# The sample rows' second norm and FFN operands made inside the first FFN pair, and their high and low parts side by side in the output and down projections

## The chip, the cores and the metric

The program runs on one core of a Trainium2 chip. The metric is the device time of one execution in microseconds (us). TensorE (PE) multiplies, VectorE (DVE), ScalarE (ACT) and GpSimd (POOL) work on tiles in on-chip memory, and SyncE (SP) issues most of the DMAs. Each engine runs its own instructions in order; semaphores order them against each other.

## The reference

One step of a one-layer encoder over 2048 prompt frames and 64 sample frames (width 1024). Each frame goes through the same chain, cut here to what matters:

```python
h = rmsnorm(x, g_mix);  z = h @ w_in            # retention heads and softmax (FoX) heads
mix = concat(ret_output(o_r, g_r), o_fox)       # 512 + 512 columns
x = x + mix @ w_out                             # output projection
h = rmsnorm(x, g_ffn)                           # the second norm
x = x + (silu(h @ w_gate) * (h @ w_up)) @ w_down   # D_FF = 2816
y = rmsnorm(x, g_final)
```

The outputs also hold the keys, values and log forget values of all frames and the retention states.

## The kernel before

Everything is float32. A product is made of two-term operands: `split` makes a high part (ACT casts to fp32r, the format that PE multiplies in one pass) and a low part (DVE subtracts), and a product is three matmuls: high by high, high by low, low by high.

The stages, in order of time:

- **Projections** (`prep`, `product`, `parts`, until about 313 us): two passes `p` over eight pairs of 128-frame tiles. `parts(p, i)` turns the queries and keys of tile `i` with PE (into the PSUM tile `tr`), splits them into `qkT`, splits the values into `vt` and stores both (`qk_d`, `v_d`). `qkT` and `vt` have one buffer each (`bufs=1`), so a tile's parts wait until the stores of the tile before have left the buffer.
- **Heads**: `r_stream` (retention; weights `w_2463` and `w_3440` for the first two heads, hidden states `hT`) runs interleaved with `m_stream` (the sample's softmax heads) and then with `f_stream` (the prompt's softmax heads; PE tiles `s`, `t`, `pv`). `run` does the interleaving: every `yield` of the one stream gives time to the other, which pays with the number that it yields. The weights of the third stage of `r_stream` are loaded and split by `mix_gen[2]`; then `p3_stream` follows in the same stream.
- **Output projection** (`p3_stream`): for each of 17 tiles (16 prompt tiles, and tile 16 with the 64 sample rows and 64 rows of padding) 48 matmuls with `mm<-w,mT`, the residual sum into `x`, the norm (`norm`: ACT squares, POOL makes the factor `r`, DVE scales into `h`), and, one tile later, `back`: eight transposes `rt<-ident,h`, copies into `hT`. After every second tile, and after tile 16 alone, `operands` makes the seven sums and differences that the FFN's products of two halves need and stores them (`h2_d`, in the trace `h_d`); for the first block they are split at once into `hb_t`. The stores wait in the list `late` and go through POOL's DMA queue.
- **FFN** (`prep`, `gu`, `down`, `finish`): three blocks of frames, `BLOCKS = ((768, 768), (0, 768), (1536, 576))`, and for each block 11 pairs `i` of 256 hidden columns. In a pair `gu(i, 0)` makes the gate half (seven products `j` of 12 matmuls `mm<-hb,w`; seven in place of eight, by sums of operands), then `down(i - 1)` the down projection of the pair before (tiles of 128 frames, twelve matmuls `dn<-wd,act` each), then `gu(i, 1)` the up half. `prep(x)` makes the weights of product `x` four products ahead; PSUM tile `b` of a product is shared by some `j`, so a later `j` waits until DVE or ACT has read the earlier one. The last block holds 512 prompt frames and the 64 sample rows: its halves are 288 columns wide, and its fifth down tile has 64 rows only. `finish` norms a tile of the result `y` and stores it.

The order on each engine is that of the code as a scheduler lays it out from the order in which the streams are emitted; pools with few buffers set who waits for whom. On SP all loads stand in one queue.

Of the kernel before, what the change touches and what calls it, by code (L numbers as in the profile page):

```python
# [9 lines left out]
F32 = mybir.dt.float32  # L10
# [6 lines left out]
D = 1024  # L17
# [21 lines left out]
def hybrid_kernel(ctx: ExitStack, tc: tile.TileContext, a: dict):  # L39
# [151 lines left out]
    with tc.tile_pool(name="p1w", bufs=1) as p1w, tc.tile_pool(name="p1", bufs=2) as p1, \  # L191
# [177 lines left out]
        def parts(p, i):  # L369
# [13 lines left out]
            qkT = p1.tile([128, 2, 4, 128], F32R, tag="qkT", name="qkT", bufs=1)  # L383
# [6 lines left out]
            vt = p1.tile([128, 4, 2, DH], F32R, tag="vt", name="vt", bufs=1)  # L390
# [116 lines left out]
        for e in range(2):  # L507
            parts(1, 2 * prev[1] + e)
# [11 lines left out]
    def r_stream():  # L520
# [160 lines left out]

    def p3_stream(last):

        m_t, mT_t, x_t, h_t, rb_t = {}, {}, {}, {}, {}
        hT_b, late = [], []
# [23 lines left out]
        def halves(i):  # L709
# [16 lines left out]
        def back(i):  # L726
# [9 lines left out]
            if i == NT - 1:  # L736
                operands(i // 2, hT[:, :, 0:NS // 2], hT[:, :, NS // 2:NS])
            elif i % 2:
                operands(i // 2, *hT_b[-2:])
            p3_done.add(i)  # L740

        def operands(j, b1, b2):

            w = b1.shape[2]
            lo, hi = slice(0, 4), slice(4, 8)
            t = p3.tile([128, D], F32, tag="h", name="t", bufs=2).rearrange("p (k t) -> p k t", k=KT)[:, :, 0:w]

            def out(n, src):
                if (0, n) in hb_t and j in range(p0, p1):
                    q = slice((j - p0) * 128, (j - p0 + 1) * 128)  # L750
                    split(hb_t[0, n][:, 0, :, q], hb_t[0, n][:, 1, :, q], src)
                    return
                stored.add(j)
                late.append(lambda: dma(h2_d[n, :, :, j * 128:j * 128 + w], src, ge))

            out(0, b1[:, lo])
            out(2, b1[:, hi])
            out(6, b2[:, hi])
            ve.tensor_tensor(t[:, lo], b2[:, lo], b1[:, lo], op=ALU.subtract)
            ve.tensor_tensor(t[:, hi], b2[:, hi], t[:, lo], op=ALU.subtract)  # L760
            ve.tensor_tensor(b2[:, lo], b2[:, hi], b2[:, lo], op=ALU.subtract)
            out(4, t[:, lo])
            out(1, t[:, hi])
            out(3, b2[:, lo])
            t4 = p3.tile([128, 4, 128], F32, tag="t4", name="t4", bufs=1)[:, :, 0:w]
            ve.tensor_tensor(t4, t[:, hi], b1[:, hi], op=ALU.subtract)
            out(5, t4)
            if j == NT // 2:
                for o in late:
                    o()  # L770

        def products(mT, c):
            ps = rps.tile([128, 512], F32, tag="mm", name="mm")
            for q in range(4):
                for k in (2 * q, 2 * q + 1):
                    for j, (u, v) in enumerate(((0, 0), (0, 1), (1, 0))):
                        te.matmul(ps, mT[:, u, k], mix_w[4 + c][:, v, k], start=k == 0 and j == 0, stop=k == 7 and j == 2)  # L777
                yield ps
# [7 lines left out]
        for c in range(2):  # L786
            for q, ps in enumerate(products(mT, c)):
# [5 lines left out]
        with tc.tile_pool(name="p3", bufs=2, reuse_waits="tile") as p3:  # L793
# [5 lines left out]
            for i in range(NT):  # L799
# [7 lines left out]
                for c in range(2):  # L807
                    for q, ps in enumerate(products(mT, c) if i else early[c:c + 1]):
# [10 lines left out]
                for o in late:  # L819
                    o()  # L820
# [695 lines left out]
```

## Time and profile before

| what | value |
|---|---|
| median of 3 runs | 2978.17 us (2974.83 to 2978.39) |
| the profiled execution | 2976.43 us, of which the span of the profile is 2974.7 us |
| granted TensorE clock | 0.99 of full speed, mean |
| PE busy | 2873.8 us of the span |
| DVE, ACT, POOL busy | 2114.5, 1308.3, 434.3 us |
| projections until | about 313 us |
| FFN from | about 1527 us |

Times in the rows are counted from the start of the span. A row of the timeline is: start, duration, engine, line, operation, output and inputs, form, count, and in brackets the idle time of the engine ahead of it and what ended that. A row of the windows is: the stretch, its length, the busy time of PE, PEld (weight loads), DVE, ACT and POOL with their counts, the granted clock, the DMA engines' busy share and their rate. Matmuls overlap in the pipeline, so what one costs in a row of them is the distance of the starts, not its own duration.

### The profile page before, as it was taken

How to read it: one execution, taken by the hardware profiler on the slowest of the kernel's cores; microseconds unless marked ns; L12 is line 12 of the kernel's file. 1: busy time of each engine (PE TensorE's matmuls, PEld its weight loads, DVE VectorE, ACT ScalarE, POOL GpSimd, SP SyncE). 2: the span in 40 equal slices, each digit the busy share in tenths (PEclk: the TensorE clock that was granted, in tenths of full speed). 3: DMA queues.
4: the chain of work that ended last, by engine and by line, in shares of the span. 5: the costliest groups of instructions: out<-in, count | busy, mean ns of one | idle time of the engine just before them, and what ended most of it. 6: DMA issues, size and time to landing. Idle time of an engine off the chain costs nothing.

```text
span 2974.7 us, 44950 instructions
## 1 busy us (share of the span) xinstructions
PE 2873.8 (97%) x16440; PEld 2591.4 (87%) x16440; DVE 2114.5 (71%) x4142; ACT 1308.3 (44%) x2765; POOL 434.3 (15%) x611
## 2 busy tenths in 40 slices
PE   7999899999999999899989999999999999999998
PEld 7999688888888888678779999998899999888887
DVE  7887644476766666766647777778777777888886
ACT  6554332265655555654333323335333333533333
POOL 2100111211111111111131011011110110211111
PEclk9999999999999999999989999999999999999999
DMA  6876633332431222554462222216222221622321
GB/s 199 271 227 189 168 106 106 102 104 72 139 90 55 72 87 87 164 157 124 143 215 85 71 58 85 70 58 203 84 85 69 59 78 52 213 86 85 86 86 61
DMA packets 408016, 338.50 MB, mean 114 GB/s; under 512 B 24138, under 2 KB 353226, under 8 KB 407794
## 3 DMA queue, kind: packets, MB, share of 16 engines
q1 hardware_dynamic: 402322, 317.07, 36.1%
q0 software_dynamic: 5472, 18.55, 1.9%
q8 instruction: 130, 2.13, 0.3%
q14 instruction: 92, 0.75, 0.1%
HBM read 255.65 MB, written 79.89 MB: 113 GB/s over the span
## 4 chain that ended last, share of the span: by engine, by line
PE 44%; DVE 3%; issue 2%; DMA 1%; POOL 1%; ACT 1%; POOLq 0%; SPq 0%; ACTq 0%; DVEq 0%
PE mm L1365 25%; PE dn L1394 16%; PE mm L777 3%; DVE w L87 1%; DMA hb<-h_d 0%; DMA raw<-w_up 0%; DVE o L1406 0%; PE rt L732 0%; DVE hb L87 0%; DVE y L1395 0%; POOL r L106 0%; POOL s L1286 0%; POOL s L1287 0%; DVE G L1338 0%; DMA o_yp<-o 0%
## 5 line engine op out<-in xcount | busy, mean ns | idle before, releaser
L1365 PE MATMUL mm<-hb,w 128*128 128x384 f32 (+1 forms) x5544 | 902.5, 324 | 15.8 <-DVE G L1338 11.9
L1365 PEld LDWEIGHTS mm<-hb,w 128*128 128x128 f32 x5544 | 894.1, 189 | 23.8 <-issue 15.2
L1394 PE MATMUL dn<-wd,act 128*128 128x512 f32 (+1 forms) x2244 | 517.6, 391 | 4.7 <-ACT act L86 2.7
L1394 PEld LDWEIGHTS dn<-wd,act 128*128 128x128 f32 (+1 forms) x2244 | 413.9, 185 | 98.1 <-ACT act L86 3.5
L662 PE MATMUL mm<-w,hT 128*128 128x512 f32 x1600 | 438.2, 407 | 9.8 <-DVE qkT L87 9.8
L1395 DVE TENSOR_TENSOR y<-y,dn 128x512 f32<-128x512 f32 (+1 forms) x374 | 255.4, 685 | 162.0 <-PE dn L1394 161.7
L662 PEld LDWEIGHTS mm<-w,hT 128*128 128x128 f32 x1600 | 285.4, 190 | 61.1 <-issue 10.5
L87 DVE TENSOR_TENSOR w<-raw,w 128x512 fp32r<-128x512 f32 (+1 forms) x350 | 302.5, 878 | 43.5 <-ACT w L86 37.9
L86 ACT CAST w<-raw 128x512 fp32r<-128x512 f32 (+1 forms) x350 | 215.9, 644 | 200.5 <-PE mm L1365 119.7
L291 PE MATMUL mm<-w,o 128*128 128x386 f32 x1260 | 239.2, 346 | 5.5 <-DVE z L302 3.9
L86 ACT CAST wd<-rawd 128x512 fp32r<-128x512 f32 x132 | 75.7, 619 | 380.2 <-PE dn L1394 377.7
L1092 ACT ACTIVATE P<-P,nm 128x512 f32<-128x512 f32 (+3 forms) x288 | 189.6, 661 | 101.4 <-DVE nm L1086 100.8
L291 PEld LDWEIGHTS mm<-w,o 128*128 128x128 f32 x1260 | 222.4, 191 | 9.5 <-DVE z L302 6.8
L1286 POOL TENSOR_TENSOR s<-raw 128x512 f32<-128x512 f32 x33 | 67.2, 2037 | 1074.2 <-DVE w L87 1040.6
L777 PE MATMUL mm<-w,mT 128*128 128x512 f32 x816 | 209.7, 405 | 6.3 <-DVE x L817 5.8
L86 ACT CAST hi<-t 128x512 fp32r<-128x512 f32 (+1 forms) x288 | 154.6, 561 | 127.9 <-PE t L1109 124.4
L87 DVE TENSOR_TENSOR lo<-t,hi 128x512 fp32r<-128x512 f32 (+1 forms) x288 | 182.8, 655 | 33.7 <-ACT hi L86 32.2
L777 PEld LDWEIGHTS mm<-w,mT 128*128 128x128 f32 x816 | 151.4, 191 | 39.3 <-DVE x L817 6.9
L1109 PE MATMUL t<-ident,P 128*128 128x128 f32 x1088 | 159.7, 275 | 6.3 <-DVE lo L87 4.9
L1125 PE MATMUL pv<-hi,V 128*128 128x256 f32 x576 | 153.2, 291 | 4.4 <-DVE o L1134 2.5
L1109 PEld LDWEIGHTS t<-ident,P 128*128 128x128 f32 x1088 | 127.1, 141 | 28.4 <-DVE lo L87 9.1
L1126 PE MATMUL pv<-lo,V 128*128 128x256 f32 x576 | 145.9, 287 | 2.4 <-DVE lo L87 1.8
(263 smaller groups left out, 3980.4 us busy)
## 6 DMA issues: line engine op xcount, KB each, us to landing
raw<-w_gate SPq DMA_DIRECT2D x66, 512.0 KB
raw<-w_up SPq DMA_DIRECT2D x66, 512.0 KB
rawd<-w_down SPq DMA_DIRECT2D x66, 512.0 KB
hT<-hT_d SPq DMA_DIRECT2D x46, 512.0 KB
x<-x_prompt SPq DMA_DIRECT2D x32, 512.0 KB
qk_d<-qkT SPq DMA_DIRECT2D x64, 256.0 KB
KA<-qk_d SPq DMA_DIRECT2D x72, 128.0 KB
V<-v_d SPq DMA_DIRECT2D x36, 256.0 KB
```

What stands on the lines that cost most here:

```text
L86: se.copy(hi, src)
L87: ve.tensor_tensor(lo, src, f32(hi), op=ALU.subtract)
L291: te.matmul(ps, o[:, u, k], w[:, v, k], start=b == j and k == 0 and m == 0, stop=j not in (0, 4) and k == 3 and m == 2, skip_group_check=True)
L662: te.matmul(ps, hT[:, u, k], w[:, v, k], start=k == 0 and j == 0, stop=k == 7 and j == len(terms) - 1)
L777: te.matmul(ps, mT[:, u, k], mix_w[4 + c][:, v, k], start=k == 0 and j == 0, stop=k == 7 and j == 2)
L1092: se.activation(v, v, AF.Exp, bias=nm, scale=-1.0, accum_out=sum_t[h, u // 4][:, i % 8, ch:ch + 1])
L1109: te.transpose(tr[:, c * 128:(c + 1) * 128], P_t[n, e, j // 2][:, k * 128:(k + 1) * 128], ident)
L1125: te.matmul(o, V, hi[:, p], start=j == 0 and c == 0, stop=False)
L1126: te.matmul(o, V, lo[:, p], start=False, stop=j == u and c == 1)
L1365: te.matmul(ps, w[:, u, k], hb_t[n, j][:, v, k, 0:hf], start=b == j and k == 0 and m == 0, stop=j not in (0, 4) and k == 3 and m == 2, ski ...
L1394: te.matmul(ps, act_t[i][e][:, u, f:f + m], w[c][:, v, e], start=e == 0 and j == 0, stop=e == 1 and j == 2)
L1395: ve.tensor_tensor(y[:, d], y[:, d], ps, op=ALU.add)
```

## The change

- The last pair's `parts` of the projections take buffers of their own (`slots`: the tiles of four `o` operands that are no longer needed) and go in the order second tile, first tile.
- The last four steps of `mix_gen[2]` each yield 1500, so that time is given back to the other stream between them.
- In the output projection tile 16 holds the high parts of its 64 rows in columns 0 to 63 and the low parts in columns 64 to 127 (`halves_beside`): two matmuls instead of three, and `add_low` adds the lower half of the PSUM tile to the upper.
- The norm, the transposes and `operands` of tile 16 leave `p3_stream`. The new `sample_operands` does them in `gu(0, 0)`, one step ahead of each of `j` = 3 to 6; it reads `x1_d` and the gain again, in six `y` tiles. The loads of `y` for the first block's results (`load_y`) follow its last step.
- In `prep(0)` the first weights are split ahead of the sums of the weights.
- In the down projection of the last block the 64-row tile holds high and low parts side by side, two matmuls instead of three; `gu` splits each result in two pieces (256 and 32 columns), `load_y` clears the lower half of `y`, `finish` adds the lower half to the upper.

```diff
-        def parts(p, i):
+        def parts(p, i, slots=None):
...
-            qkT = p1.tile([128, 2, 4, 128], F32R, tag="qkT", name="qkT", bufs=1)
+            if slots is None:
+                qkT = p1.tile([128, 2, 4, 128], F32R, tag="qkT", name="qkT", bufs=1)
+                vt = p1.tile([128, 4, 2, DH], F32R, tag="vt", name="vt", bufs=1)
+            else:
+                qkT, vt = (p1w.tile([128, 2, 4, 128], F32R, tag=f"o{n}", name="last") for n in slots)
+                vt = vt[:, 0].rearrange("p h (s d) -> p h s d", s=2)
...
-        for e in range(2):
-            parts(1, 2 * prev[1] + e)
+        for e in (1, 0):
+            parts(1, 2 * prev[1] + e, (2 * e, 2 * e + 1))
...
         for _ in range(4):
             next(mix_gen[2])
+            yield 1500
         yield from p3_stream([lambda f=f: f(prev) for f in (step_T, step_A, step_O, step_M)])
...
-                split(mT[:, 0, s], mT[:, 1, s], m[:, s])
+                if i == 16:
+                    halves_beside(mT[:, 0, s], m[:, s])
+                else:
+                    split(mT[:, 0, s], mT[:, 1, s], m[:, s])
...
-        def products(mT, c):
+        def products(mT, c, i):
+            terms = ((0, 0), (0, 1), (1, 0))[0:2 if i == 16 else 3]
...
+                    if i == 16:
+                        add_low(ps, p3.tile([128, 512], F32, tag="t4", name="t16", bufs=1)[0:NS])
                     ve.tensor_tensor(x[:, d], ps, x[:, d], op=ALU.add)
-                norm(i, x)
-                for o in late:
-                    o()
-                late.clear()
-            yield from back(NT - 1)
+                if i < 16:
+                    norm(i, x)
+                else:
+                    dma(x1_d[SEQ:TP], x, ge)
+                write_late()
...
             if j == 0:
...
+                if x == 0:
+                    split(o[:, 0], o[:, 1], r0[:, lo])
                 en = ge if s else ve
...
-            full = [(t0 + 128 * m, 128, m // 2 * 128 + m % 2 * (hf + tail // 2)) for m in range(nt // 128)]
+            full = [(t0 + 128 * m, 128, m // 2 * 128 + m % 2 * (hf + 2 * tail)) for m in range(nt // 128)]
...
+            if m < 128:
+                ge.memset(y[m:2 * m], 0.0)
             dma(y[0:m], x1_d[t:t + m])
...
-                split(o[:, 0, c:c + hf - tail], o[:, 1, c:c + hf - tail], g[:, 0:hf - tail])
+                split(o[:, 0, c:c + full], o[:, 1, c:c + full], g[:, 0:full])
                 if tail:
-                    split(o[:, 0, hf:c], o[:, 1, hf:c], g[:, hf - tail:hf])
+                    c = full + tail * (q % 2)
+                    split(o[:, 0, c:c + tail], o[:, 0, c + 2 * tail:c + 3 * tail], g[:, full:hf])
...
+                terms = ((0, 0), (0, 1), (1, 0))[0:3 if m == 128 else 2]
...
-            y = y_t.pop(t)[0:n]
+            yy = y_t.pop(t)
+            y = yy[0:n]
             o = fw.tile([128, D], F32, tag="rawd", name="o", bufs=2)[0:n]
+            if n < 128:
+                se.copy(o, yy[n:2 * n])
+                ve.tensor_tensor(y, y, o, op=ALU.add)
...
+        def sample_operands():
+
+            x, g, h, hT, t, t4 = (fw.tile([128, D], F32, tag="y", name="y", bufs=6) for _ in range(6))
+            dma(x, x1_d[SEQ:TP])
+            dma(g, a["norm_ffn_gain"].to_broadcast([128, D]))
+            yield
+            r = rms_scale(fw, x, h, 128, 2)
+            ve.scalar_tensor_tensor(h, x, r, g, op0=ALU.mult, op1=ALU.mult)
+            yield
+            hT = hT.rearrange("p (k t) -> p k t", k=KT)
+            for g in range(2):
+                tr = ps4.tile([128, 512], F32, tag="dn", name="tr").rearrange("p (k t) -> p k t", k=4)
+                for k in range(4):
+                    te.transpose(tr[:, k], h[:, (4 * g + k) * 128:(4 * g + k + 1) * 128], ident)
+                se.copy(hT[:, 4 * g:4 * g + 4], tr)
+            yield
+            operands(NT // 2, hT[:, :, 0:NS // 2], hT[:, :, NS // 2:NS], t, t4[:, 0:512])
+            for t, m, _ in tiles(0):
+                load_y(t, m)
+            yield
...
-        for t, m, _ in tiles(0):
-            load_y(t, m)
+        first = sample_operands()
...
             for j in gu(i, 0):
+                if i == 0 and j >= 3:
+                    next(first)
```

`operands` moves out of `p3_stream` unchanged in what it computes, with the two scratch tiles as arguments.

On SP, where the projections end and the heads begin, before (`vt` and `qkT` are the buffers of the parts, `rot`, `tri`, `nmask` and `self` are constants, `raw<-w_in` are the last two quarters of the weights `w_3440`, `o_lfp` the output of the log forget values):

```order
L48 DMA cg<-c_gam 128x16
L48 DMA rot<-c_rot 128x128
L48 DMA raw<-w_in 128x2x256
L48 DMA qk_d<-qkT 128x4x128 x2
L48 DMA v_d<-vt 128x4x128
L48 DMA raw<-w_in 128x2x256 x3
L48 DMA rot<-c_rot 128x128
L48 DMA qk_d<-qkT 128x4x128 x2
L48 DMA v_d<-vt 128x4x128
```

The same place now:

```order
L48 DMA qk_d<-last 128x4x128 x4
L48 DMA rmask<-c_rmask 128x512
L48 DMA cg<-c_gam 128x16
L48 DMA o_lfp<-lf 128x16x8
L48 DMA o_lfs<-lf 64x8
L48 DMA tri<-c_tri 128x128
L48 DMA nmask<-c_nmask 128x64
L48 DMA self_3413<-c_sel 40x512
L48 DMA rot<-c_rot 128x128
L48 DMA raw<-w_in 128x2x256 x4
```

The last stores of the parts moved ahead of the constants, and the four weight loads moved behind the store of the forget values and four constants.

On PE at the same place, before (`tr` the last turns of the parts, `s<-ident,A` turns for the sample's heads, `w_2463` and `w_3440` the two weight tiles of the first retention tile):

```order
L375 MATMUL tr<-ident,z 128x128 x8
L884 MATMUL s<-ident,A_941 8x128 x4
L662 MATMUL mm<-w_2463,hT 128x512 x6
L884 MATMUL s<-ident,A_941 8x128 x4
L662 MATMUL mm<-w_2463,hT 128x512 x11
L884 MATMUL s<-ident,A_941 8x128 x4
L662 MATMUL mm<-w_2463,hT 128x512
```

The same place now:

```order
L375 MATMUL tr<-ident,z 128x128 x8
L899 MATMUL s<-ident,A_941 8x128 x4
L666 MATMUL mm<-w_2463,hT 128x512 x6
L899 MATMUL s<-ident,A_941 8x128 x4
L666 MATMUL mm<-w_2463,hT 128x512 x18
L666 MATMUL mm<-w_3440,hT 128x512 x11
L899 MATMUL s<-ident,A_941 8x128 x4
```

Eleven matmuls of the second weight tile moved ahead of the turns `s<-ident,A`.

On PE where the output projection ends and the FFN begins, before (`w_14160` is the second weight tile of the projection, `rt` the turns of `h`; the rows `rt` behind the first FFN row are those of tile 16):

```order
L777 MATMUL mm<-w_14160,mT 128x512 x18
L732 MATMUL rt<-ident,h 128x128 x4
L777 MATMUL mm<-w_14160,mT 128x512 x4
L732 MATMUL rt<-ident,h 128x128 x4
L777 MATMUL mm<-w_14160,mT 128x512 x2
L1365 MATMUL mm<-hb,w 128x384 x12
L732 MATMUL rt<-ident,h 128x128 x8
L1365 MATMUL mm<-hb,w 128x384 x240
```

The same place now (`tr<-ident,y` are the turns of tile 16):

```order
L789 MATMUL mm<-w_13989,mT 128x512 x16
L789 MATMUL mm<-w_14160,mT 128x512 x12
L774 MATMUL rt<-ident,h 128x128 x4
L789 MATMUL mm<-w_14160,mT 128x512 x4
L774 MATMUL rt<-ident,h 128x128 x4
L1389 MATMUL mm<-hb,w 128x384 x84
L1453 MATMUL tr<-ident,y 128x128 x8
L1389 MATMUL mm<-hb,w 128x384 x168
```

The turns of tile 16 moved behind the whole gate half of the first pair, and tile 16 has 32 matmuls where it had 48. On SP the six loads of `y` moved with them:

```order
L48 DMA raw<-w_up 128x8x128 x2
L48 DMA y<-x_d 128x1024
L48 DMA raw<-w_gate 128x8x128 x2
L48 DMA y<-norm_ffn_gain 128x1024
L48 DMA rawd<-w_down 128x2x512 x2
L48 DMA y<-x_d 128x1024 x6
L48 DMA raw<-w_up 128x8x128 x2
```

The six loads stood directly behind the first two `raw<-w_up` before; now they stand between the first `rawd<-w_down` and the second pair's `raw<-w_up`, and a load of the sample's rows and one of the gain stand ahead.

More of the change, by code (lines that the diff above doesn't have):

```diff
@@ L676, in r_stream, with write_late, operands, out @@
             next(mix_gen[2])
+            yield 1500
         yield from p3_stream([lambda f=f: f(prev) for f in (step_T, step_A, step_O, step_M)])
     f_done = set()
+    def write_late():
+        for o in late:
+            o()
+        late.clear()
+    def operands(j, b1, b2, t, t4):
+        w = b1.shape[2]
+        lo, hi = slice(0, 4), slice(4, 8)
+        t = t.rearrange("p (k t) -> p k t", k=KT)[:, :, 0:w]
+        t4 = t4.rearrange("p (k t) -> p k t", k=4)[:, :, 0:w]
+        def out(n, src):
+            if (0, n) in hb_t and j in range(p0, p1):
+                q = slice((j - p0) * 128, (j - p0 + 1) * 128)
+                split(hb_t[0, n][:, 0, :, q], hb_t[0, n][:, 1, :, q], src)
+                return
+            stored.add(j)
+            late.append(lambda: dma(h2_d[n, :, :, j * 128:j * 128 + w], src, ge))
+        out(0, b1[:, lo])
+        out(2, b1[:, hi])
+        out(6, b2[:, hi])
+        ve.tensor_tensor(t[:, lo], b2[:, lo], b1[:, lo], op=ALU.subtract)
+        ve.tensor_tensor(t[:, hi], b2[:, hi], t[:, lo], op=ALU.subtract)
+        ve.tensor_tensor(b2[:, lo], b2[:, hi], b2[:, lo], op=ALU.subtract)
+        out(4, t[:, lo])
+        out(1, t[:, hi])
+        out(3, b2[:, lo])
+        ve.tensor_tensor(t4, t[:, hi], b1[:, hi], op=ALU.subtract)
+        out(5, t4)
+        if j == NT // 2:
+            write_late()
     def p3_stream(last):
         m_t, mT_t, x_t, h_t, rb_t = {}, {}, {}, {}, {}
-        hT_b, late = [], []
+        hT_b = []
         def load_m(i):
@@ L735, in back @@
             hT_b.append(hT)
[L736 to L739, printed above, removed]
+            if i % 2:
+                operands(i // 2, *hT_b[-2:], p3.tile([128, D], F32, tag="h", name="t", bufs=2),
+                         p3.tile([128, 512], F32, tag="t4", name="t4", bufs=1))
             p3_done.add(i)
[L742 to L768, printed above, removed]
-                for o in late:
-                    o()
-        def products(mT, c):
+        def products(mT, c, i):
+            terms = ((0, 0), (0, 1), (1, 0))[0:2 if i == 16 else 3]
             ps = rps.tile([128, 512], F32, tag="mm", name="mm")
@@ L775, in products @@
                 for k in (2 * q, 2 * q + 1):
-                    for j, (u, v) in enumerate(((0, 0), (0, 1), (1, 0))):
-                        te.matmul(ps, mT[:, u, k], mix_w[4 + c][:, v, k], start=k == 0 and j == 0, stop=k == 7 and j == 2)
+                    for j, (u, v) in enumerate(terms):
+                        te.matmul(ps, mT[:, u, k], mix_w[4 + c][:, v, k], start=k == 0 and j == 0,
+                                  stop=k == 7 and j == len(terms) - 1)
                 yield ps
@@ L786, in p3_stream @@
         for c in range(2):
[L787 removed]
+            for q, ps in enumerate(products(mT, c, 0)):
                 if q % 2 == 0:
```

36 lines of the change are left out of this document (19 added, 17 removed).

## The prediction

> **What bounds the kernel now.** I read the page first, its busy times and its chain, then the groups of waits, then the timeline of the four places that the change touches.
>
> ```profile
> PE 2873.8 (97%) x16440; PEld 2591.4 (87%) x16440; DVE 2114.5 (71%) x4142; ACT 1308.3 (44%) x2765; POOL 434.3 (15%) x611
> PE 44%; DVE 3%; issue 2%; DMA 1%; POOL 1%; ACT 1%; POOLq 0%; SPq 0%; ACTq 0%; DVEq 0%
> ```
>
> PE is busy for 2873.8 of 2974.7 us and has the largest part of the chain. So time can be won in two ways only: by fewer matmuls, or out of the 100.9 us in which PE idles. Everything off PE counts where it makes PE wait, and at the very end.
>
> **The last parts of the projections.** The only wait of the first retention matmuls stands here:
>
> ```profile
> 323.36 2.90 PE L662 MATMUL mm<-w,hT 128*128 128x512 f32 x6 [9.85 <-DVE qkT L87]
> 316.53 1.60 SPq L48 DMA_DIRECT2D qk_d<-qkT  x2
> 321.14 0.38 ACT L384 ACTIVATE qkT<-tr 128x256 fp32r<-128x256 f32 x1 [4.89 <-DVE p L848]
> 318.49 1.16 DVE L87 TENSOR_TENSOR w<-raw,w 128x1024 fp32r<-128x1024 f32 x1
> 318.77 2.27 SPq L48 DMA_DIRECT2D raw<-w_in  x3
> 323.03 1.05 ACT L86 CAST w<-raw 128x1024 fp32r<-128x1024 f32 x1 [0.34 <-DMA raw<-w_in]
> 325.95 0.38 SPq L48 DMA_DIRECT2D o_lfp<-lf  x1
> 326.38 1.30 SPq L48 DMA_DIRECT2D o_lfs<-lf  x1
> 328.37 0.47 SPq L48 DMA_DIRECT2D tri<-c_tri  x1
> 313.00:323.00 10.00, 0.51 (x5) 0.17 (x2) 9.14 (x20) 2.85 (x7) 5.47 (x11) 0.71 0.97 269
> 325.00:327.00 2.00, 2.00 (x8) 1.26 (x8) 1.89 (x4) 1.40 (x2) 0.00 (x0) 0.50 0.97 256
> 327.00:329.00 2.00, 2.00 (x9) 1.64 (x9) 1.87 (x12) 0.57 (x1) 0.00 (x0) 0.87 0.66 63
> ```
>
> PE idles from 313.51 to 323.36. The single `qkT` is stored at 316.53, refilled only from 321.14, and PE comes after its split; meanwhile DVE works at the sample's softplus (`p`) and the weights. With buffers of their own the last parts (about 0.4 us each on DVE and ACT, as the 0.38 of the copy) should be through at about 316.5: PE starts 6.9 us earlier. But the order now puts the last four loads of `w_3440` behind `o_lfp`, which waits for `lf`, the end of the softplus. `lf` comes earlier too: 2.4 us of weight splits (two like the 1.16) move behind it and about 0.9 of DVE's 10 us were idle, so `o_lfp` goes at about 322.6. Behind it stand five small transfers (`o_lfs` 1.30, the constants 0.4 to 0.5 like `tri`, about 3.1 us), so the loads go at about 326; from issue to the cast it took 323.03 - 318.77 = 4.3 us, with cast and split (1.05 + 1.16) the third quarter is ready at about 332. PE gets there after 36 matmuls and 20 small turns, 316.5 + 36 x 0.235 + 1.8 + 2 for a half clock = about 329. A wait of some 2.5 us comes back: 6.9 - 2.5 = 4.4, **taken -4.5**; ends 0 (the loads land so late that all is given back) and -9.5 (no wait is left).
>
> **The four yields.** They move projection matmuls against the end of the prompt's softmax heads.
>
> ```profile
> 1200.00:1230.00 30.00, 21.90 (x129) 17.86 (x128) 25.57 (x64) 22.25 (x48) 3.54 (x6) 0.94 0.57 171
> 1230.00:1300.00 70.00, 61.18 (x335) 49.85 (x334) 41.13 (x104) 34.72 (x84) 6.85 (x14) 0.98 0.55 151
> 1229.28 0.40 PE L777 MATMUL mm<-w,mT 128*128 128x512 f32 x1
> L1126 PE MATMUL pv<-lo,V x576: 272/281/562, 601.3 to 1394.3; 128*128 128x256 f32 x189, 128*128 128x128 f32 x3
> ```
>
> PE idles 8.1 us of the first stretch (27%) and 8.8 of the second; the first projection matmul comes at 1229.28 and the softmax runs to 1394.3. The order still mixes the two streams and puts the first projection matmuls a little later. I see no reason for a sign: **taken 0**, ends -8 (half of the 16.9 idle) and +6 (three quarters of one more stretch of 8.1).
>
> **Output projection and start of the FFN.**
>
> ```profile
> 1502.89 10.50 PE L777 MATMUL mm<-w,mT 128*128 128x512 f32 x44
> 1527.58 2.25 PE L1365 MATMUL mm<-hb,w 128*128 128x384 f32 x12
> 1533.11 1.11 PE L732 MATMUL rt<-ident,h 128*128 128x128 f32 x4 [3.28 <-DVE h L722]
> 1534.94 1.11 PE L732 MATMUL rt<-ident,h 128*128 128x128 f32 x4 [0.72 <-ACT hT L733]
> 1537.11 1.65 PE L1365 MATMUL mm<-hb,w 128*128 128x384 f32 x4 [1.06 <-ACT U L1368]
> 1539.43 2.93 PE L1365 MATMUL mm<-hb,w 128*128 128x384 f32 x8 [0.68 <-ACT w L86]
> 1541.52 9.38 PE L1365 MATMUL mm<-hb,w 128*128 128x384 f32 x50
> 1553.84 16.35 PE L1365 MATMUL mm<-hb,w 128*128 128x384 f32 x77 [2.94 <-DVE G L1338]
> 1541.60 0.99 SPq L48 DMA_DIRECT2D raw<-w_up  x2
> 1562.80 0.99 SPq L48 DMA_DIRECT2D raw<-w_up  x2
> 1553.80:1556.00 2.20, 2.16 (x7) 2.19 (x8) 1.56 (x3) 1.90 (x4) 0.00 (x0) 0.50 1.15 317
> ```
>
> Tile 16 loses 16 matmuls; 44 take 10.50 us and overlap a little at the end, so 0.235 each: -3.8. From 1527.58 to 1541.52, 13.9 us, PE does 24 FFN matmuls and the eight turns, with 3.28 + 0.72 + 1.06 + 0.68 us of waits. Now the turns go and with them the wait for the norm: 24 x 0.188 (9.38 / 50) = 4.5 us, the wait for `U` and for the next split as before (1.74), and about 1.8 for DVE, which has the halves' sum and the residual of tile 16 (two additions like the y additions, 0.7) ahead of the splits: 8.0. That is -5.9. The eight turns come later, at 1.1 us (the two rows show 1.11 each, at half clock): +1.1. The stores and loads come later as well. The second `raw<-w_up` was issued at 1562.80; now it stands behind six loads of `y`, which wait for the sample's stores, at an estimate some 8 us later and about when the second pair needs its first split: +1. The first `raw<-w_up` (1541.60) keeps its place behind POOL's stores, so the wait of 2.94 stays. Cover of the sample's norm and sums: the gate half's matmuls; DVE carries them, and it is DVE that PE waits for at 1553.84. Sum -3.8 - 5.9 + 1.1 + 1 = **-7.6**; ends -11 and -3. The split of the first weights ahead of their sums goes with it, at nothing of its own; 0.68 (`ACT w`) is its most.
>
> The clock is a cost of its own: after 9.85 us of waiting it stood at 0.50 until about 327.5, after 2.94 us it stood at 0.50 too, but not everywhere:
>
> ```profile
> 2602.00:2604.00 2.00, 2.00 (x10) 1.62 (x11) 2.00 (x4) 0.00 (x0) 0.00 (x0) 1.00 0.00 0
> 2601.82 8.49 PE L1394 MATMUL dn<-wd,act 128*128 128x512 f32 x36 [2.01 <-DVE y L1395]
> ```
>
> A wait of 2.01 us left it at 1.00. So I take half clock for waits of 2.9 and more and full clock at 2.0. The Trainium skill's page "TensorE: Matmul & The Clock Gate", section "Part 1: The HAM clock gate (the "warmup" mystery)", has the gate close after an idle window of about 3.4 us. The row of 2.94 contradicts it as a limit on one wait. By the rule, a new wait of 2.5 to 2.9 us costs only itself and the total would be about 2 us lower; by the rows it can cost up to 2 us more.
>
> **The down projection of the last block.**
>
> ```profile
> 2669.33 13.82 PE L1394 MATMUL dn<-wd,act 128*128 128x512 f32 x60
> 2682.99 20.70 PE L1365 MATMUL mm<-hb,w 128*128 128x288 f32 x156
> 2704.07 1.82 PE L1365 MATMUL mm<-hb,w 128*128 128x288 f32 x12 [0.39 <-DVE G L1338]
> 2689.83 0.45 DVE L87 TENSOR_TENSOR act<-G,act 128x288 fp32r<-128x288 f32 x1
> 2692.62 0.53 DVE L87 TENSOR_TENSOR act<-G,act 128x256 fp32r<-128x256 f32 x2
> L1394 PEld LDWEIGHTS dn<-wd,act 128*64 128x64 f32 x132 | 17.7, 134 | 11.9
> L1394 PEld LDWEIGHTS dn<-wd,act 128*128 128x128 f32 x2112 | 396.1, 188 | 86.2 <-ACT act L86 3.5 <-DVE y L1395 2.4 <-DVE act L87 0.2
> ```
>
> 60 matmuls stand between 2669.33 and 2682.99: 0.2277 each. Four fewer per pair are 0.91 us; ten of the eleven pairs lie in this row's manner between PE's other work, the last is counted with the end: -9.1. The narrow tile's weights get 128 columns: 88 loads of 188 ns are 16.5 us, where 132 of 134 were 17.7, and both hide under 0.2277. Two more results per pair are split in two pieces (0.53 where 0.45 stood): 0.16 us of DVE per pair. It lies in the up half; where DVE is late (PE's 0.39) it can reach PE, so +0.5 over all of 1.8 at most. **-8.6**, ends -9.5 and -5 (a wait of 0.4 more in every pair). The POOL `memset` of half of `y` stands ahead of a load that is needed a block's first pair later; POOL is 15% busy: 0, and with its cover gone at most about 1.3, what the 64x1024 below takes on DVE.
>
> **The end.**
>
> ```profile
> 2967.39 1.06 ACT L102 ACTIVATE o<-y 64x1024 f32<-64x1024 f32 x1 [3.34 <-DMA o_yp<-o]
> 2969.46 1.28 DVE L1406 SCALAR_TENSOR_TENSOR o<-y,r,gfin 64x1024 f32<-64x1024 f32 x1 [2.92 <-POOL r L106]
> ```
>
> The last tile's square waits for the buffer `o` (3.34 us, for a store) and nothing hides what follows. A copy like 1.06 and an addition like 1.28 come behind that wait: +2.34, with hand-overs **+2.4**. Its ends are +1 (the four fewer matmuls of the last pair, 0.9, bring part of it forward) and +3.
>
> **Sum.** -4.5 + 0 - 7.6 - 8.6 + 2.4 = -18.3. On the profiled execution's 2976.43 us this is 2958.1. The median of the runs shown is 2978.17, 1.7 higher, so I say 2959, between the two.
>
> **Rivals.**
>
> 1. More comes from the yields. PE's 16.9 us of idling at the end of the softmax are halved: -8, time 2951, and with better ends elsewhere 2941 to 2951. For it: projection matmuls are ready work there. Against it: the first ones come later than before.
>
> 2. The start of the FFN turns into a new wait. The sample's norm and sums (1.28 for a scaling of 64x1024, and seven sums) go on DVE in just the stretch where PE waits 2.94 us for DVE; and SP's queue holds back `raw<-w_up`, each us of lateness a us of PE, with half clock behind it. 3 us at the first, 3 at the second, with 2 for the clock: +8, time 2967; 2965 to 2972. For it: DVE is the releaser in both waits. Against it: the same DVE work stood in the 14 us before.
>
> 3. About the same, 2972 to 2984: the terms of the down projection and of tile 16 stand (-12.4), but the loads of `w_3440` give back more than the buffers won (+4.5 over 0) and the FFN's start too. Time 2974.
>
> 4. Slower, over 2984, by one mechanism: with time given back to the softmax between the last steps, the projection's matmuls come so late that the softmax runs alone. Alone it idles 27% (1200 to 1230). To eat the 18.3 us and 7 more takes 25 / 0.27 = 92 us alone: no projection matmul before 1229 + 92 = 1321. Against it: the order still interleaves them from the beginning.
>
> 5. That the change doesn't do what it says: a wait stays at the `tr` of the parts, since their PSUM tiles and DVE are the old ones. Then -4.5 becomes 0: 2963, inside the range.
>
> **How the numbers follow.** A run of this kernel tells 0.2%, 6 us, from no change, so "same" is 2972 to 2984. The forecast, 2951 to 2965: 0.57. Rival 1: 0.11. Rival 2: 0.18. Rival 3: 0.10. Rival 4: 0.04. Rival 5 lies in the forecast. Faster is 0.57 + 0.11 + 0.18 = 0.86. The range, 2949 to 2971, leaves out most of rival 1, rivals 3 and 4, and a little of rival 2: about 0.2.
>
> **What the profile after would show.** The wait of 9.85 us at the first retention matmul falls to about 3, and a new one of 2 to 3 stands behind the first half of `w_3440`, released by the DVE or ACT split. The two stretches from 1200 keep about 17 us of idling. No turn of `h` stands between the FFN's first matmuls; the first 24 take about 8 us. A `dn` row of one pair has 56 matmuls in 12.75 us. At the end a copy and an addition stand ahead of the last square. I am wrong if the new operands make PE wait over 5 us for `G` or `w` in the first two pairs, or if the softmax's end shifts by more than 8 us.

## The result and the profile after

The changed kernel took 2956.1 us (median, 2955.22 to 2956.78), the kernel before 2978.28 us beside it: a ratio of 0.9924, 95% interval 0.9908 to 0.994. The forecast was 2959, range 2949 to 2971. The profiled execution took 2955.22 us, its span is 2953.4 us; that is 21.3 us less than the span before.

The page after, busy times and chain:

```profile
PE 2859.6 (97%) x16380; PEld 2584.8 (88%) x16380; DVE 2121.6 (72%) x4167; ACT 1310.6 (44%) x2790; POOL 436.8 (15%) x612
PE 42%; DVE 5%; issue 2%; DMA 2%; POOL 1%; ACT 0%; SPq 0%; POOLq 0%; DVEq 0%; ACTq 0%
```

PE is busy 14.2 us less and idle 93.8 us instead of 100.9. The 60 matmuls that are gone (16 and 44) make about two thirds of the gain. Of the 7.1 us less idling, 5.8 lie between 1200 and 1515 us (21.1 us before, 15.4 now), where PE's idle time differs by as much between runs with the same yields, as the experiments show. So this trace alone doesn't show that the change won them.

Where the heads begin, the timeline after, and then the window 313 to 345 of before and of after:

```profile
314.57 2.46 PE L666 MATMUL mm<-w,hT 128*128 128x512 f32 x6 [1.63 <-DVE x L853]
324.28 1.19 PE L666 MATMUL mm<-w,hT 128*128 128x512 f32 x4 [0.23 <-DVE w L87]
329.37 1.20 PE L899 MATMUL s<-ident,A 128*8 128x128 f32 x8 [0.83 <-DVE arow L903]
333.09 0.66 PE L575 MATMUL rt<-ident,qk 128*128 128x128 f32 x4 [1.44 <-POOL qk L551]
319.75 0.40 SPq L48 DMA_DIRECT2D o_lfp<-lf  x1
323.23 1.91 SPq L48 DMA_DIRECT2D raw<-w_in  x4
322.46 1.74 DVE L87 TENSOR_TENSOR w<-raw,w 128x1024 fp32r<-128x1024 f32 x1
330.55 1.22 DVE L87 TENSOR_TENSOR w<-raw,w 128x1024 fp32r<-128x1024 f32 x1
```

```profile
313.00:345.00 32.00, 22.09 (x128) 15.86 (x126) 23.84 (x54) 12.39 (x22) 7.50 (x14) 0.84 0.73 193
```

```profile
313.00:345.00 32.00, 26.91 (x148) 19.07 (x149) 23.51 (x52) 14.10 (x25) 9.62 (x14) 0.95 0.54 146
```

The wait of 9.85 us is one of 1.63, and PE starts 8.8 us earlier. But a row of small waits follows: for the split of `w`, for `arow` (the turns of `A`), for POOL's rotation. The split that PE waits for at 324.28 was begun at 322.46, before the last four loads were issued at 323.23; theirs is begun at 330.55, and no row shows PE waiting for it. In the 32 us PE idles 5.1 us where it idled 9.9, so nearly half of the gain is gone within some 20 us.

Where the FFN begins, the timeline after; the last row is the first down projection of before:

```profile
1516.23 2.33 PE L1389 MATMUL mm<-hb,w 128*128 128x384 f32 x12
1525.01 1.65 PE L1389 MATMUL mm<-hb,w 128*128 128x384 f32 x4 [6.44 <-ACT U L1392]
1527.93 14.70 PE L1389 MATMUL mm<-hb,w 128*128 128x384 f32 x68 [1.28 <-ACT w L86]
1543.59 29.42 PE L1389 MATMUL mm<-hb,w 128*128 128x384 f32 x168
1572.85 16.51 PE L1419 MATMUL dn<-wd,act 128*128 128x512 f32 x72
1523.87 0.58 ACT L95 COPY t<-mm 64x512 f32<-64x512 f32 x1 [6.64 <-DMA h_d<-t]
1519.62 0.92 POOL L48 DMA_DIRECT2D h_d<-t  x1
1523.21 2.36 SPq L48 DMA_DIRECT2D raw<-w_up  x2
```

```profile
1587.90 16.50 PE L1394 MATMUL dn<-wd,act 128*128 128x512 f32 x72
```

From the FFN's first matmul to the first down projection it is 56.6 us (1572.85 - 1516.23) instead of 60.3 (1587.90 - 1527.58). The turns of `h` and the wait for the norm are gone, and so is the wait of 2.94 us; but a new wait of 6.44 us stands for the copy of `U`. ACT names its cause one row on: the copy in `add_low` (L95) stands ahead of that of `U` in ACT's queue, and it waits 6.64 us for the store `h_d<-t`. Its scratch tile has the tag `t4`, one buffer, and that buffer still holds the last operand of the prompt's frames, whose store POOL issued at 1519.62. The first `raw<-w_up` went out 7.0 us behind the FFN's first matmul (1523.21); before it was 14.0 us (1541.60 - 1527.58).

The softmax of the prompt ended earlier, at 1384.4 us instead of 1394.3:

```profile
L1141 PE MATMUL pv<-lo,V x576: 272/281/583, 599.7 to 1384.4; 128*128 128x256 f32 x189, 128*128 128x128 f32 x3
```

The last block's down projection, and the end:

```profile
2652.71 12.90 PE L1419 MATMUL dn<-wd,act 128*128 128x512 f32 x56
2688.29 12.89 PE L1419 MATMUL dn<-wd,act 128*128 128x512 f32 x56
2651.05 1.82 PE L1389 MATMUL mm<-hb,w 128*128 128x288 f32 x12 [0.45 <-DVE G L1360]
2925.43 13.05 PE L1419 MATMUL dn<-wd,act 128*128 128x512 f32 x56
2943.40 1.04 ACT L1431 COPY o<-y 64x1024 f32<-64x1024 f32 x1 [2.85 <-DMA o_yp<-o]
2944.48 1.22 DVE L1432 TENSOR_TENSOR y<-y,o 64x1024 f32<-64x1024 f32 x1 [1.40 <-ACT o L1431]
2945.79 1.06 ACT L102 ACTIVATE o<-y 64x1024 f32<-64x1024 f32 x1 [1.34 <-DVE y L1432]
```

A pair takes 35.58 us (2688.29 - 2652.71). PE's wait for `G` grew from 0.39 to 0.45. The last copy still waits for a store, then copy, addition and square follow one another with nothing beside them.

### The profile page after: what moved, and what is told of

Read it like the earlier page. It is cut to its first block, busy times and chain, and to the rows that moved or that the text cites. A ratio compares the mean times of both kernels' runs of the same rounds, so it can differ in the third digit from the quotient of the medians.

```text
span 2953.4 us, 44888 instructions
## 1 busy us (share of the span) xinstructions
PE 2859.6 (97%) x16380; PEld 2584.8 (88%) x16380; DVE 2121.6 (72%) x4167; ACT 1310.6 (44%) x2790; POOL 436.8 (15%) x612
## 4 chain that ended last, share of the span: by engine, by line
PE 42%; DVE 5%; issue 2%; DMA 2%; POOL 1%; ACT 0%; SPq 0%; POOLq 0%; DVEq 0%; ACTq 0%
PE mm L1389 23%; PE dn L1419 16%; PE mm L789 3%; DVE w L87 2%; DMA hb<-h_d 1%; DMA raw<-w_up 0%; DVE act L87 0%; DVE G L1365 0%; DVE o L1436 0%; DMA o_yp<-o 0%; DVE hb L87 0%; DVE y L1421 0%; DVE raw L1311 0%; PE rt L774 0%; POOL r L106 0%
## 5 line engine op out<-in xcount | busy, mean ns | idle before, releaser
L1389 PEld LDWEIGHTS mm<-hb,w 128*128 128x128 f32 x5544 | 893.7, 189 | 27.3 <-issue 13.5
L1419 PE MATMUL dn<-wd,act 128*128 128x512 f32 x2200 | 506.9, 390 | 3.4 <-ACT act L86 2.9
L1419 PEld LDWEIGHTS dn<-wd,act 128*128 128x128 f32 x2200 | 411.8, 188 | 88.7 <-ACT act L86 3.8
L1421 DVE TENSOR_TENSOR y<-y,dn 128x512 f32<-128x512 f32 x374 | 255.4, 686 | 156.5 <-PE dn L1419 155.9
L789 PE MATMUL mm<-w,mT 128*128 128x512 f32 x800 | 202.6, 401 | 2.9 <-DVE x L832 2.5
```

What stands on the lines that cost most here:

```text
L1389: te.matmul(ps, w[:, u, k], hb_t[n, j][:, v, k, 0:hf], start=b == j and k == 0 and m == 0, stop=j not in (0, 4) and k == 3 and m == 2, ski ...
L1419: te.matmul(ps, act_t[i][e][:, u, f:f + 128], w[c][:, v, e], start=e == 0 and j == 0, stop=e == 1 and j == len(terms) - 1)
L1421: ve.tensor_tensor(y[:, d], y[:, d], ps, op=ALU.add)
```

## The experiments

Beside the next runs the kernel before took 2983 to 2985 us, some 6 us more than beside the first, so kernels are compared by their ratio to it. The intervals are about 0.13% wide on each side, 4 us; where less matters, the stretches of the trace decide. The changed kernel was run again for that:

> The changed kernel once more, on the chip of the next three, so that they are compared with it there. It takes 0.9908 to 0.994 of the time of the kernel before, as it did. In the profile the wait for U at the FFN's first matmuls is 6.4 us again, and no wait of 2.9 us for G follows it.

It took 2965.83 us, 0.9939 (0.9926 to 0.9952). The wait for `U` was 6.42 us, and a wait of 1.46 us stood at the sample's turns. The two ratios of the changed kernel are 0.0015 apart, 4.5 us, with intervals that overlap. The differences given below are from the second, unless the first is named.

### The parts: back to single buffers

```diff
-        for e in (1, 0):
-            parts(1, 2 * prev[1] + e, (2 * e, 2 * e + 1))
+        for e in range(2):
+            parts(1, 2 * prev[1] + e)
```

> The changed kernel with the last pair's parts in the old single buffers and the old order. Theory 1 (most of the 8.8 us won at the first retention matmul are given back within 150 us, by the waits of the turns and of POOL and a clock drop at about 468): it takes 1.5 to 3 us more than the changed one, 2957.5 to 2959. Rival (the 8.8 us stay, and the traces differ for another reason): 2963 to 2965, with the wait of 9.8 us back at the first retention matmul in both cases.

2969.58 us, 0.9942 (0.9929 to 0.9955). In the timeline of this kernel and then of the changed one run again: the last turns of the projections, and the third `pv<-hi` of the prompt's softmax (the row that the expectations call the first `pv`; the first stands about 4.9 us earlier in each of these traces).

```profile
314.19 1.01 PE L375 MATMUL tr<-ident,z 128*128 128x128 f32 x7 [0.80 <-DVE z L304]
326.05 2.90 PE L666 MATMUL mm<-w,hT 128*128 128x512 f32 x6 [10.41 <-DVE qkT L87]
607.92 0.39 PE L1140 MATMUL pv<-hi,V 128*128 128x256 f32 x1 [0.22 <-ACT hi L86]
```

```profile
314.65 0.55 PE L375 MATMUL tr<-ident,z 128*128 128x128 f32 x3 [0.60 <-DVE z L306]
604.75 0.39 PE L1140 MATMUL pv<-hi,V 128*128 128x256 f32 x1 [0.23 <-ACT hi L86]
```

From the end of the turns to the `pv` it is 607.92 - 315.20 = 292.7 us with the single buffers and 604.75 - 315.20 = 289.55 with the new ones. The kernel before has 292.2 there, the one with the yields alone 292.5, the changed one of the first measurement 291.1 and all others with the new buffers, bar the next one, 288.9 to 289.8. So the parts are worth about 3 us (1.1 in the first trace) out of a wait that shrank by 8.2, and theory 1 holds by this stretch. The total time (0.0003 above the changed kernel) can't tell 3 us.

### The weight loads ahead of the stores of the forget values

```diff
 # end of log_forget
-        dma(a["o_lfp"]..., lf[:, 0:16])
-        dma(a["o_lfs"], lf[0:64, 16])
 # m_stream, behind the loop over the turns of A
+        dma(a["o_lfp"]..., lf[:, 0:16])
+        dma(a["o_lfs"], lf[0:64, 16])
```

> The changed kernel with the stores o_lfp and o_lfs moved behind the last four loads of w_3440. Theory 1 (what is given back after the first retention matmul comes from the turns of A, which wait for DVE, and from POOL's rotation, not from the weights): the waits for the split of w at the first retention matmuls (0.2 to 1.6 us) go, and under 1 us of time. Rival (the loads behind o_lfp are what gives back 4 us of the 7 won): 3 to 4 us less at the softmax's first pv matmul, 286 us after the end of the last tr, where the changed kernel takes 289.5.

2964.75 us, 0.9932 (0.992 to 0.9945); 288.4 us from the turns to the `pv`, 1.2 less than the changed kernel run again. The waits for `arow` and for POOL's rotation are still there (0.43, 0.23, 0.83 and 1.67 us). That for `w` is 0.30 us, where it was 1.17; but with the stores ahead it was 0.23 and 0.24 in two traces whose first six matmuls were slow as well (2.46 and 2.80 us, here 2.54), so the move of the loads needn't be what shortened it. So the loads that the prediction named give back 1 us at most, and the rival, with 3 to 4, is out. That the turns and the rotation give back more is read from their waits; no run takes these away.

### The yields

```diff
-            next(mix_gen[2])
-            yield 1500
+            next(mix_gen[2])
```

> The changed kernel without the four yields of 1500; all else as changed. Theory 1 (the yields win time at the end of the softmax): up to the first projection matmul the two traces of before and after stand 1.3 us apart, at the FFN's start 11.35, of which 3.8 are the fewer matmuls of tile 16; so 6.2 us are the yields', and this kernel takes about 2962 us, with PE idle in 1200 to 1300 back at about 17 us. Rival (the end of the softmax is better because the streams before it ended in another phase, through the parts): this kernel stays at 2956 and PE's idle time there stays near 12.

2969.0 us, 0.9946 (0.9934 to 0.9959): 0.0007, 2 us, above the changed kernel run again, inside both intervals, but 0.0022, 6.6 us, above its first measurement, which is theory 1's number. PE's idle time from 1200 to 1300 is 13.2 us, nearer the rival's 12 than the 17 of theory 1. And the yields alone, in the kernel before:

> The kernel before, with the four yields of 1500 and nothing else of the change. Theory 1 (the yields alone win some 3 to 6 us between 1200 and 1440): 0.998 to 0.999 of the kernel before. Rival (they win only together with the parts, which bring the streams into another phase): within 1.5 us of the kernel before.

2983.91 us, 0.9995 (0.9985 to 1.0005). So over 4.5 us are excluded for the yields alone. In the changed kernel they are worth 2 or 6.6 us, by which of its two measurements is taken, and these differ by 4.5 us themselves: it isn't settled. The rows tell why. Two waits each of the kernel without the yields, of the kernel before with them, and the one that stands at its place before:

```profile
1303.55 0.94 PE L1123 MATMUL t<-ident,P 128*128 128x128 f32 x4 [2.30 <-DVE lo L87]
1435.95 11.60 PE L788 MATMUL mm<-w,mT 128*128 128x512 f32 x42 [3.73 <-DVE x L831]
```

```profile
1309.06 1.12 PE L1110 MATMUL t<-ident,P 128*128 128x128 f32 x4 [4.33 <-DVE lo L87]
1431.91 10.05 PE L778 MATMUL mm<-w,mT 128*128 128x512 f32 x42 [1.34 <-DVE x L818]
```

```profile
1429.39 11.59 PE L777 MATMUL mm<-w,mT 128*128 128x512 f32 x42 [3.50 <-DVE x L817]
```

With the yields the wait for `x` in the output projection is 0.6 to 2.2 us in eleven runs and 4.04 in one; without them it was 3.50 and 3.73, with half clock behind it (0.50 from 1431 to 1433 us before). But another wait, in the softmax near 1305, is 2.2 to 4.5 us with them, and 1.04 and 2.30 without. PE's idle time from 1200 to 1515 is 21.1 and 20.1 us without the yields and 15.4 to 21.8 with them. The 6 us that the first two traces differ by here are within what this stretch varies by from run to run (6.4 us with the same yields); what sets it in a run is open. The longer stretch from the third `pv<-hi` to the FFN's first matmul varies even more: with the same parts and yields it takes 912.7 us in the first trace of the changed kernel and 915.6 to 925.6 us in nine others, without the yields 926.9 us.

### The scratch of add_low

```diff
-  add_low(ps, p3.tile([128, 512], F32, tag="t4", name="t16", bufs=1)[0:NS])
+  add_low(ps, p3.tile([128, 4, 128], F32, tag="rb", name="t16")[0:NS].rearrange("p k t -> p (k t)"))
```

> The changed kernel, with the scratch of add_low in two buffers that are free (rb) in place of t4. Theory 1 (the wait of 6.44 us at the FFN's first matmuls is the store of t4, which must leave the buffer before add_low may write it): that wait falls under 2 us, and the kernel takes 4 to 6 us less than the changed one, 2950 to 2952. Rival (the copy of U and the weights' sums wait for something else as well, the sample's residual or DVE's queue): the wait stays above 4 us or comes back as a wait for w, and the time is 2955 to 2957.

2961.3 us, 0.9918 (0.9905 to 0.9931). The timeline of this kernel at the FFN's start, on PE, POOL and SP:

```profile
1530.22 2.36 PE L1389 MATMUL mm<-hb,w 128*128 128x384 f32 x12
1533.15 0.61 PE L1389 MATMUL mm<-hb,w 128*128 128x384 f32 x2 [0.57 <-ACT U L1392]
1551.07 3.71 PE L1389 MATMUL mm<-hb,w 128*128 128x384 f32 x12 [2.65 <-DVE G L1360]
1544.65 1.31 POOL L1306 TENSOR_TENSOR s<-raw 128x512 f32<-128x512 f32 x1 [9.62 <-ACT G L1361]
1537.23 1.25 SPq L48 DMA_DIRECT2D raw<-w_up  x2
```

The wait for `U` fell from 6.4 to 0.57 us: the store of `t4` was its cause. From the first FFN matmul to the first down projection it is 54.6 us instead of 56.6 (53.5 to 55.1 in five runs with the own scratch, 56.3 to 57.2 in six without). So 2 us came of nearly 6, since the wait for `G` is back with 2.65 us and half clock behind it: PE now reaches that matmul before the first `raw<-w_up` is used. In the changed kernel the wait for `t4` had hidden it. The ratio is 0.0021, 6 us, below the changed kernel run again and 0.0006, 2 us, below its first measurement, so the time doesn't decide; by the trace the rival holds in part.

POOL sums the up weights 7.4 us behind the issue of their load. Are the sums the limit, or the load?

```diff
-                en = ge if s else ve
+                en = ge if s and i else ve
```

> The run with the own scratch for add_low, and the sums of the first pair's up weights made by DVE instead of POOL (3 x 0.69 us for 3 x 1.3). Theory 1 (with the wait for t4 gone, PE's 2.05 to 2.65 us for G stand behind POOL's sums, which the split of w and so DVE's next work wait for): that wait falls under 1.3 us, the stretch from the first FFN matmul to the first down projection from 54 us to 52.5, and the kernel takes 1 to 2 us less than with the scratch alone. Rival (the load of w_up itself is the limit, it lands 7 us after its issue): the wait stays over 1.8 us.

2960.11 us, 0.9916 (0.9902 to 0.993). PE's wait there:

```profile
1547.60 3.74 PE L1389 MATMUL mm<-hb,w 128*128 128x384 f32 x12 [2.29 <-DVE G L1360]
```

It is 2.29 us, between the 2.05 and 2.65 of two runs with POOL's sums, so theory 1's number is out and the rival's, over 1.8, is met. DVE's first sum waits for the load, 8.1 us behind its issue at 1534.74. Below it stand POOL's first sum and the wait of the last run of this document, which has POOL's sums:

```profile
1542.83 0.69 DVE L1306 TENSOR_TENSOR s<-raw 128x512 f32<-128x512 f32 x1 [3.42 <-DMA raw<-w_up]
1532.20 1.31 POOL L1306 TENSOR_TENSOR s<-raw 128x512 f32<-128x512 f32 x1 [10.25 <-DMA raw<-w_up]
1538.61 3.74 PE L1389 MATMUL mm<-hb,w 128*128 128x384 f32 x12 [3.27 <-DVE G L1360]
```

So the load is a limit with either engine. But the sums count too: with POOL's, PE waited 2.05, 2.65 and 3.27 us when the first sum came 6.6, 7.4 and 8.1 us behind the issue; with DVE's, 1.86 and 2.29 us when it came 8.0 and 8.1 us behind. At the same age of the load DVE's sums save about 1 us, part of what theory 1 had, and a later load hid it here.

### Tile 16 normed in the output projection

```diff
-                if i < 16:
-                    norm(i, x)
-                else:
-                    dma(x1_d[SEQ:TP], x, ge)
+                norm(i, x)
                 write_late()
+            yield from back(NT - 1)
...
-                if i == 0 and j >= 3:
-                    next(first)
```

> The changed kernel, but the norm, the turns and the operands of tile 16 stay in the output projection, as before; its two matmuls, the down projection, the parts and the yields are as changed. Theory 1 (moving them won only the difference of two waits: from the FFN's first matmul to the first down projection it was 60.32 us before and 56.62 after): this stretch takes about 60 us, and the kernel 3 to 4 us more than the changed one. Rival (the wait for t4 goes away too, since add_low comes long ahead of the FFN's matmuls that wait for it, and the move won nothing): 56 to 58 us in the stretch and no difference.

2974.57 us, 0.9966 (0.9954 to 0.9978), 0.0027 above the changed kernel, some 8 us. PE and ACT there:

```profile
1536.79 1.11 PE L774 MATMUL rt<-ident,h 128*128 128x128 f32 x4 [10.86 <-DVE h L764]
1559.51 32.97 PE L1388 MATMUL mm<-hb,w 128*128 128x384 f32 x180 [3.69 <-DVE G L1359]
1531.24 0.58 ACT L95 COPY t<-mm 64x512 f32<-64x512 f32 x1 [6.64 <-DMA h_d<-t]
```

Neither theory had it: the wait for `t4` stays (6.64 us) and the norm comes behind it, so PE waits 10.86 us where it waited 3.28 before, and the stretch to the first down projection takes 68.7 us. Two matmuls in place of three for tile 16 bring the wait for `t4` with them, and the move takes it off the norm.

### The old down projection

The functions `tiles`, `load_y`, `gu`, `down` and `finish` as before.

> The changed kernel with the down projection of the last block as before: three matmuls for the 64-row tile, no copy and addition at the end. Theory 1 (four matmuls of 0.2277 us in each of ten pairs, and a shorter last pair, less 2.2 us at the end): 6.8 us more than the changed one, about 2963. Rival (the two extra splits of each pair already cost on DVE what PE shows as its 0.46 us of waiting, so that undoing gives some back): under 5 us more, 2958 to 2961.

2972.03 us, 0.9957 (0.9945 to 0.997): 0.0018 above the changed kernel, 5.4 us, between the two expectations (0.0033, 9.8 us, above the first measurement). The trace is sharper. Two down projections of this kernel, and its last:

```profile
2628.72 13.83 PE L1413 MATMUL dn<-wd,act 128*128 128x512 f32 x60
2665.13 13.83 PE L1413 MATMUL dn<-wd,act 128*128 128x512 f32 x60
2944.69 13.90 PE L1413 MATMUL dn<-wd,act 128*128 128x512 f32 x60
```

A pair takes 36.41 us here (2665.13 - 2628.72) and 35.58 in the changed kernel, 0.83 less: four matmuls of 0.2277 are 0.91, less 0.06 for the longer wait for `G` (0.45 beside 0.39) and 0.02 that no row names. From the first matmul of the last down projection to the end of the span it is 25.7 us (2970.4 - 2944.69), in the changed kernel 28.0 (2953.4 - 2925.43): the end costs 2.3 us.

### The end

In the last block, `o` in `y` buffers, with the own scratch:

```diff
+            if t >= BLOCKS[-1][0]:
+                o = fw.tile([128, D], F32, tag="y", name="o", bufs=6)[0:n]
+            else:
                 o = fw.tile([128, D], F32, tag="rawd", name="o", bufs=2)[0:n]
```

> The changed kernel with the own scratch for add_low (as in the run with rb) and, in the last block, the result tiles o in free y buffers, so that the last copy need not wait for a store. Theory 1 (at the end the copy waited 2.85 us for the store of o, and the path is copy, addition, square, factor, scaling): it ends 2 to 3 us earlier than with the scratch alone, 3 to 5 us under the changed kernel. Rival (the last matmuls and DVE's additions of the tile are the path, so that the copy then waits for y): under 1 us from this.

2960.22 us, 0.9924 (0.9911 to 0.9936). From the last down projection's first matmul to the end 26.5 us, 1.5 less than 28.0: less than the 2 to 3 of theory 1. The copy now waited 2.29 us for DVE's additions to `y`: DVE was close behind the store. The ratio, no lower than with the scratch alone (0.9918), doesn't show the 1.5 us.

The 64-row tile third of five in the last pair, with the scratch and the sums on DVE:

```diff
+            todo = tiles(n)
+            if i == NB * NP - 1:
+                todo = [todo[q] for q in (0, 2, 4, 1, 3)]
-            for t, m, f in tiles(n):
+            for t, m, f in todo:
```

> The run before this one, and in the last pair the 64-row tile is third of the five, so that its copy and addition have matmuls beside them and the last tile is one of 128 rows. Theory 1 (the end is a chain of store, copy, addition, square, factor, scaling behind the last matmul): from the first matmul of the last down projection to the end it takes 25 to 26 us where the changed kernel takes 28.0, and the whole 0.991 of the kernel before. Rival (DVE has additions of y and scalings for all of that time and moves the copy's work only): over 27 us.

2959.49 us, 0.9917 (0.9903 to 0.993), and 27.3 us at the end: the rival's number, but not for its reason. ACT's last square:

```profile
2949.27 1.06 ACT L102 ACTIVATE o<-y 128x1024 f32<-128x1024 f32 x1 [4.20 <-DMA o_ys<-o]
```

It waits 4.20 us for a store. So the last run has the scratch, the order of the tiles, and `y` buffers for the first three `o`:

> The changed kernel with the own scratch for add_low; in the last pair the 64-row tile is third of the five, and the result tiles o of the first three stand in free y buffers, so that no square waits for a store. Theory 1 (with the tail inside, the wait of 4.20 us for the store of o_ys kept the end late): from the first matmul of the last down projection to the end it takes about 24 us where the changed kernel takes 28.0 and the run with the tail inside 27.3; the whole 0.990 to 0.9915 of the kernel before. Rival (DVE's additions and scalings fill the time anyway): 26 us or more.

2953.48 us, 0.9900 (0.9885 to 0.9916), with the lowest ratio of all; its interval overlaps that of the changed kernel of the first measurement and lies below that of the second. The first matmul of the down projection, and ACT's last square:

```profile
2921.63 12.90 PE L1422 MATMUL dn<-wd,act 128*128 128x512 f32 x56
2937.28 1.04 ACT L102 ACTIVATE o<-y 128x1024 f32<-128x1024 f32 x1
```

No square waits for a store any more, and the end takes 24.9 us (2946.5 - 2921.63), 3.1 less than in the changed kernel.

## Why the prediction was right

The sum was -18.3 us; the first two traces differ by 21.3, and the ratio of the second measurement, 0.9939, is worth 18.2 us. The terms, each by the runs that bear on it:

| term | predicted | measured | from |
|---|---|---|---|
| parts | -4.5 | -3 | end of the turns to `pv`, with and without the buffers |
| yields | 0 | not settled, 0 to -6.6 | ratios with and without |
| output projection and FFN's start | -7.6 | -3.8 - 3.7 = -7.5 | 16 matmuls; 60.3 to 56.6 us |
| down projection | -8.6 | -9.0 | first to last down projection of the last block, 356.3 and 347.3 us |
| end | +2.4 | +2.3 | old down projection beside the changed one |

Without the yields the measured terms make -17.2. The same by place, in us, for the trace of before, the first of the changed kernel and that of the run again:

| stretch | before | changed | run again |
|---|---|---|---|
| end of the turns to the third `pv<-hi` | 292.2 | 291.1 | 289.6 |
| to the FFN's first matmul | 922.3 | 912.7 | 919.7 |
| to the first down projection | 60.3 | 56.6 | 56.8 |
| to the last block's first down projection | 1004.7 | 1005.3 | 1005.1 |
| to its last down projection | 356.3 | 347.3 | 347.4 |
| to the end of the span | 25.8 | 28.0 | 28.0 |

- **The total** owes something to luck. In the first trace the parts gave 1.1 us of the 4.5, and the stretch behind them, which holds the yields, gave 9.7, of which tile 16 explains 3.8. The other 5.9 us belong to no term of the sum; nine other traces with the same code there are 3 to 13 us longer. The prediction's own sign of being wrong, a softmax end shifted by more than 8 us, is in this trace (1394.3 to 1384.4) and not in that of the run again (1392.1). Nor did the two stretches from 1200 keep their 17 us of idling: they have 11.8 us, in the run again 12.5.
- **Down projection and end** were right in size and mechanism. They are the terms in which a matmul, a copy and an addition stand alone on the path and have rows of their own. Ten pairs at the 0.83 us of the rows make 8.3; what the other 0.7 is stays open.
- **The parts**: the step that failed is "A wait of some 2.5 us comes back", for the last four loads. PE waited 0.2 to 1.7 us for `w`, and in the first trace this was for a split begun before those loads were issued. What was left out is that PE, now early, meets DVE and POOL in the same work as before, the splits of `arow` and the rotation: 1.85 and 1.44 us of waits in the changed kernel. The range's end of 0 holds it.
- **The FFN's start** was right in its sum by errors that cancel. The first 24 matmuls were to take 8.0 us, with "the wait for `U` and for the next split as before"; they took 14.4 (the 25th starts at 1530.65), for the store of `t4`, whose buffer the prediction did not follow. Before they took 14.6, and not the 13.9 that the prediction read: at 1541.52 two of the 24 were still to come. So the -5.9 was worth 0.2. What won most of the 3.7 was a wait that the prediction kept: "the wait of 2.94 stays" was wrong with the wait for `t4` in place and right without it: with an own scratch 2.65 us of it came back. Rival 2 named the place of the new wait, but not its cause: SP's queue did not hold the first `raw<-w_up` back, and the new wait took the place of an old one.
- **The yields** at 0 hold as far as the runs tell, with ends about as wide as the stretch was seen to vary.
- The four matmuls at 0.2277 us, the 60-matmul row becoming one of 56, and the copy and addition ahead of the last square stand as foretold. The "about 3" at the first retention matmul was 1.63, and PE started 8.8 us earlier instead of 6.9.

## What to carry to other kernels

A wait taken away on the bound engine is worth only the distance to the next thing that engine needs: here 8.2 us of waiting gave 3, and 5.9 us gave 2. Follow the buffer of every tile that a change adds, down to the store that last read it; one shared tag made the largest new wait of this change. Removed matmuls on the path pay by count times their spacing, so put them first in the sum. And before a gain in one trace is credited to a change, look at the same stretch in traces of other runs with the same code: here one of 920 us varied by 13.

## What the runs showed of the hardware

The clock after one and the same wait differs between runs. PE waited 1.63 us ahead of the first retention matmul in all runs with the new buffers. The first six matmuls, in the changed kernel and in the one with the old down projection, and the clock behind them (windows of the one and of the other):

```profile
316.08 1.63 PE L666 MATMUL mm<-w,hT 128*128 128x512 f32 x6 [1.63 <-DVE x L853]
```

```profile
316.00:318.00 2.00, 2.00 (x8) 1.35 (x7) 1.79 (x7) 1.02 (x2) 0.00 (x0) 0.50 1.15 345
```

```profile
316.08:317.70 1.62, 1.62 (x8) 1.23 (x9) 1.52 (x4) 1.16 (x2) 0.00 (x0) 1.00 1.11 333
```

2.46 us at half clock in the one, 1.63 at full clock in the other. Of the eleven runs with the new buffers four have 2.46 to 2.88 us for these six matmuls, seven 1.63 or 1.64. The same at 468 us: two waits of 0.74 and 0.88 us left the clock at 0.59 from 468 to 472 in the changed kernel and cost about 1.7 us, while 0.92 and 0.88 before left it at 1.00. A wait of 2.05 us for `G`, in the run with `o` in `y` buffers, left 0.51 (1544 to 1546 us), where the prediction's row of 2.01 us left 1.00. So the prediction's reading, half clock from 2.9 us and full clock at 2.0, was wrong: in these runs no length of a single wait is a threshold. The drops at 316 and 468 us cost 1 to 2 us each.

The Trainium skill, page "TensorE: Matmul & The Clock Gate", section "Part 1: The HAM clock gate (the "warmup" mystery)", says that the window of about 3.4 us is free-running, so that the same kernel differs from run to run. The rows agree that it differs. Its table lets the clock fall after at least one idle window of that length. If this means 3.4 us without a matmul, the rows contradict it: the clock fell behind a wait of 1.63 us (with two of 0.6 us in the 4 us ahead of it), and behind two that together were 1.62 us.
